# Quadrant moves of four tiles at once instead of two, with an order of transfers made for it

## The chip, the cores and the metric

One core of one Trainium2 chip. The metric is device microseconds of the whole kernel, as the median of its runs; "span" is the profiled stretch from the first to the last instruction, some 1.9 us shorter.

## The reference

```python
# x (16, 512, 1024), weight (1024, 768), add_value (16, 512, 768), all float32
def reference(x, weight, scale, add_value):
    return (scale * np.matmul(x, weight) + add_value).astype(np.float32)
```

Flattened, x has 8192 rows: 64 tiles of 128 rows. Each tile needs its x transposed and rounded to bf16, sixteen matmuls, and one VectorE instruction that scales the product and adds.

## The kernel before

SyncE issues all transfers in the order of one list. `x` are loads of x into 16 slots, `w` the weight, `a` loads of add_value into 32 slots, `o` stores of the results from the same 32 slots; the numbers are first tile and count.

```python
STREAM = [
    ("x", 0, 3), ("w", 0, 2), ("w", 2, 2), ("x", 3, 1), ("w", 4, 4), ("a", 0, 8),
    ("x", 4, 4), ("x", 8, 8), ("a", 8, 8), ("x", 16, 8), ("a", 16, 8), ("x", 24, 8),
    ("a", 24, 8), ("o", 0, 8), ("x", 32, 8), ("o", 8, 8), ("a", 32, 8), ("x", 40, 8),
    ("o", 16, 8), ("a", 40, 8), ("x", 48, 8), ("o", 24, 8), ("a", 48, 8), ("x", 56, 8),
    ("o", 32, 8), ("a", 56, 8), ("o", 40, 8), ("o", 48, 8), ("o", 56, 5), ("o", 61, 3),
]
```

From tile 14 on, x is not transposed on TensorE. ScalarE and GpSimd move blocks of 32 partitions to other partitions and round to bf16 on the way ("quadrant moves", two tiles at a time); one VectorE stream transpose then turns the 32 x 32 blocks.

```python
    def move_pair(t0, half):
        ...
        for b in range(4):
            for a, move in ((2 * half, nc.scalar.copy), (2 * half + 1, nc.gpsimd.tensor_copy)):
                move(moved[t0][32 * b:32 * b + 32, :, a, :],
                     src[32 * a:32 * a + 32, :, b, :])
        ...
    def turn_moved(t0):
        xt = xt_pool.tile([P, 2, KC, P], fp32, tag="xt")
        ...
        nc.vector.transpose(
            xt.rearrange("p i c m -> p (i c m)"),
            moved.pop(t0).bitcast(fp32).rearrange("p c a k -> p (c a k)"))
    ...
    def step():
        t = done["step"]
        if t < T - 1:
            for j in range(KJ):
                if j == KJ // 2:
                    if t + 1 not in in_pair:
                        transpose(t + 1)          # PE transposes, evacuated by VectorE
                    cast_to(min(t + AHEAD, done["x"] - 1))
                    for half in range(2):
                        if in_pair.get(t + 6 - half) == t + 6 - half:
                            move_pair(t + 6 - half, half)
                product(t, j, BOTH)
            finish(t, BOTH[0], 0, N)              # out = scale * product + add, in the add slot
            if in_pair.get(t + 4) == t + 4:
                turn_moved(t + 4)
    ...
    def added(t):                                 # tiles 0 to 2: their scaled product waits for add
        nc.vector.tensor_add(
            ao[:, t, :], ao[:, EARLY_AT + t, :], ao[:, t, :])
```

## Time and profile before

Median 210.29 us of three runs (210.13 to 210.51), span 208.4 us.

| From the page of the kernel before | |
|---|---|
| PE busy | 177.1 us (85%) |
| ScalarE busy, of which moves | 129.9 us (62%), 123.2 us |
| GpSimd busy, of which moves | 135.2 us (65%), 121.7 us |
| VectorE busy | 104.1 us (50%) |
| Share of the 16 DMA engines' span | 97.9%, for 87.03 MB |

How to read it: a share of busy time is an average, so the slices and the windows are needed to see whether a resource is full all the time or only in places. The lines themselves stand in the prediction below. "Issue to landing" is the time from SyncE's issue of a transfer until its landing is reported; where it is much longer than the bytes need, the transfer stood in a queue. The queue is "dry" when nothing is left in it. The "granted clock" is the share of its full speed at which TensorE was let run, as the profile records it.

### The profile page before, as it was taken

The page shows a single profiled execution, that of the slowest core. Times are in us where ns is not written, and L with a number is a line of the kernel's source. Part 1 is how long each engine was busy: PE and PEld are TensorE (multiplying, and loading weights), DVE is VectorE, ACT ScalarE, POOL GpSimd, SP SyncE. Part 2 cuts the span into 40 slices and gives each one's busy share as a digit, 9 for nine tenths or more (in the row PEclk, how much of TensorE's full clock was granted, in tenths as well). Part 3 has the DMA queues.
Part 4 walks back from the last instruction along what each step waited for, and adds up shares of the span by engine and source line. Part 5 has one row for each costly group of instructions (what it writes and reads, how often), then busy time and mean ns, then how long its engine had stood idle before and what let it go on. Part 6 is the DMA issues. An engine that isn't in the chain of part 4 may idle for free.

```text
span 208.4 us, 2843 instructions
## 1 busy us (share of the span) xinstructions
PE 177.1 (85%) x1059; PEld 108.4 (52%) x1080; DVE 104.1 (50%) x113; ACT 129.9 (62%) x210; POOL 135.2 (65%) x219
## 2 busy tenths in 40 slices
PE   0498339999999999999999999999959996799930
PEld 0355125666666666666666666666626563456510
DVE  0514713555675555566666645475054651555620
ACT  2421100540299999997999559992899919996000
POOL 1310051428699999999999759993899939997000
PEclk9999958999999999999999999999999999999995
DMA  6999999999999999999999999999999999999994
GB/s 229 413 440 448 420 459 406 440 453 415 402 464 434 413 415 425 458 415 428 415 439 451 407 436 425 450 428 407 439 426 437 453 404 426 434 437 425 423 414 187
DMA packets 4461, 87.21 MB, mean 418 GB/s; under 512 B 480, under 2 KB 480, under 8 KB 1120
## 3 DMA queue, kind: packets, MB, share of 16 engines
q1 hardware_dynamic: 4448, 87.03, 97.9%
q8 instruction: 8, 0.13, 0.2%
q14 instruction: 5, 0.04, 0.0%
HBM read 61.87 MB, written 25.17 MB: 418 GB/s over the span
## 4 chain that ended last, share of the span: by engine, by line
DMA 44%; PE 38%; POOL 10%; SPq 1%; issue 1%; DVE 1%; POOLq 0%; DVEq 0%
PE mm L170 36%; DMA out_dram<-ao 17%; DMA ao<-in_add_value_dram 15%; DMA xs<-in_x_dram 12%; POOL va L110 9%; PE tp L149 2%; DVE ao L178 1%; SPq L93 1%; SPq L250 1%; POOL xb L139 1%; SPq L256 0%; POOLq L139 0%; DVEq L178 0%
## 5 line engine op out<-in xcount | busy, mean ns | idle before, releaser
L170 PE MATMUL mm<-w_bf,xt 128*128 128x512 bf16 (+1 forms) x1003 | 170.6, 327 | 8.3 <-DVE ao L178 6.0
L110 ACT CAST va<-xs 32x512 bf16<-32x512 f32 x200 | 123.2, 616 | 46.0 <-DMA xs<-in_x_dram 43.5
L170 PEld LDWEIGHTS <-xt 128*128 128x128 bf16 x1024 | 101.0, 99 | 74.8 <-issue 5.5
L110 POOL CAST va<-xs 32x512 bf16<-32x512 f32 x200 | 121.7, 608 | 20.8 <-DMA xs<-in_x_dram 11.9
L178 DVE SCALAR_TENSOR_TENSOR ao<-mm,ao 128x768 f32<-128x768 f32 (+2 forms) x62 | 57.2, 935 | 40.3 <-PE mm L170 34.0
L119 DVE STREAM_TRANSPOSE xt<-va 128x1024 f32<-128x1024 f32 x25 | 31.1, 1244 | 29.5 <-POOL va L110 29.0
L139 POOL CAST xb<-xs 128x1024 bf16<-128x1024 f32 x11 | 11.2, 1043 | 29.4 <-DMA xs<-in_x_dram 21.8
L149 PE MATMUL tp<-identity,xb 128*128 128x128 f32 x56 | 10.2, 317 | 14.5 <-DVE xb L135 7.7
L149 PEld LDWEIGHTS tp<-identity,xb 128*128 128x128 f32 x56 | 7.7, 163 | 16.4 <-issue 7.7
L157 DVE COPY xt<-tp 128x1024 bf16<-128x1024 bf16 x10 | 6.9, 688 | 10.8 <-PE tp L149 10.8
L157 ACT COPY xt<-tp 128x512 bf16<-128x512 bf16 (+1 forms) x7 | 4.1, 655 | 9.2 <-PE tp L149 9.2
L97 DVE CAST w_bf<-ao 128x768 bf16<-128x768 f32 x8 | 4.0, 555 | 4.9 <-DMA ao<-in_weight_dram 4.9
L135 DVE CAST xb<-xs 128x512 bf16<-128x512 f32 x3 | 1.9, 695 | 7.1 <-DMA xs<-in_x_dram 7.1
L137 POOL CAST xb<-xs 128x512 bf16<-128x512 f32 x2 | 1.6, 835 | 5.9 <-DMA xs<-in_x_dram 5.9
L137 ACT CAST xb<-xs 128x512 bf16<-128x512 f32 x1 | 0.6, 619 | 5.1 <-DMA xs<-in_x_dram 5.1
L237 DVE TENSOR_TENSOR ao<-ao 128x768 f32<-128x768 f32 x3 | 2.7, 953 | 1.1 <-DMA ao<-in_add_value_dram 1.1
L206 DVE TENSOR_SCALAR ao<-mm 128x768 f32<-128x768 f32 x2 | 1.8, 953 | 2.5 <-PE mm L170 2.5
L137 ACT ACT_TABLE_LOAD x1 | 1.3, 1283 | 0.7 <-PEq L281 0.7
L203 ACT ACTIVATE ao<-mm 128x768 f32<-128x768 f32 x1 | 0.8, 817 | 0.0
masks.py:197 POOL MEMSET identity<- 128x128 f32 x1 | 0.2, 205 | 0.3 <-POOLq L281 0.3
masks.py:199 POOL TENSOR_SCALAR_AFFINE_SELECT identity<-identity 128x128 f32<-128x128 f32 x1 | 0.3, 293 | 0.1
L281 POOL MEMSET const-float32-0.0<- 128x1 f32 x1 | 0.1, 98 | 0.2 <-issue 0.2
(3 smaller groups left out, 0.3 us busy)
## 6 DMA issues: line engine op xcount, KB each, us to landing
xs<-in_x_dram SPq DMA_DIRECT2D x7, 4096.0 KB, 23.9
ao<-in_add_value_dram SPq DMA_DIRECT2D x8, 3072.0 KB, 31.1
out_dram<-ao SPq DMA_DIRECT2D x7, 3072.0 KB, 31.3
xs<-in_x_dram SPq DMA_DIRECT2D x1, 2048.0 KB, 24.4
out_dram<-ao SPq DMA_DIRECT2D x1, 1920.0 KB, 9.9
xs<-in_x_dram SPq DMA_DIRECT2D x1, 1536.0 KB, 6.4
ao<-in_weight_dram SPq DMA_DIRECT2D x2, 768.0 KB, 8.5
ao<-in_weight_dram SPq DMA_DIRECT2D x1, 1536.0 KB, 13.2
```

The source lines that it names most:

```text
L93: nc.sync.dma_start(ao[:, s:s + n, :].rearrange("p (c r) n -> p c (r n)", r=2), w_v[:, j // 2:(j + n) // 2, :])
L97: nc.vector.tensor_copy(w_bf[:, j + i, :], ao[:, s + i, :])
L110: move(moved[t0][32 * b:32 * b + 32, :, a, :], src[32 * a:32 * a + 32, :, b, :])
L119: nc.vector.transpose(xt.rearrange("p i c m -> p (i c m)"), moved.pop(t0).bitcast(fp32).rearrange("p c a k -> p (c a k)"))
L137: other(xb[:, K // 2:K], src[:, K // 2:K])
L139: nc.gpsimd.tensor_copy(xb, src)
L149: nc.tensor.transpose(tp[:, c, :], pairs[:, c * P:(c + 1) * P], identity)
L157: evacuate(xt_tiles[t][:, c:c + q, :].bitcast(bf16), tp[:, c:c + q, :].bitcast(bf16))
L170: nc.tensor.matmul(mm_tiles[t, cols[0]][:, n0:n1], lhs(t, j), w_bf[:, j, n0:n1], start=(j == 0), stop=(j == KJ - 1))
L178: nc.vector.scalar_tensor_tensor(a, mm_tiles[t, part][:, n0:n1], float(scale), a, op0=mybir.AluOpType.mult, op1=mybir.AluOpType.add)
L237: nc.vector.tensor_add(ao[:, t, :], ao[:, EARLY_AT + t, :], ao[:, t, :])
L250: nc.sync.dma_start(xs[:, k:k + n, :], rows(x_v, s, n))
```

## The change

The intent: the same bytes moved by half as many, twice as long instructions (each has a fixed part that is then paid half as often), x slots that come free in fours, and a list of 31 transfers that brings x earlier against add and out and splits the last load of x and the stores at the end anew. One buffer of moved tiles goes (three of two tiles become two of four).

```diff
--- before.py
+++ after.py
@@ -10,11 +10,12 @@
 
 
 STREAM = [
-    ("x", 0, 3), ("w", 0, 2), ("w", 2, 2), ("x", 3, 1), ("w", 4, 4), ("a", 0, 8),
-    ("x", 4, 4), ("x", 8, 8), ("a", 8, 8), ("x", 16, 8), ("a", 16, 8), ("x", 24, 8),
-    ("a", 24, 8), ("o", 0, 8), ("x", 32, 8), ("o", 8, 8), ("a", 32, 8), ("x", 40, 8),
-    ("o", 16, 8), ("a", 40, 8), ("x", 48, 8), ("o", 24, 8), ("a", 48, 8), ("x", 56, 8),
-    ("o", 32, 8), ("a", 56, 8), ("o", 40, 8), ("o", 48, 8), ("o", 56, 5), ("o", 61, 3),
+    ("x", 0, 3), ("w", 0, 2), ("w", 2, 2), ("x", 3, 1), ("w", 4, 4), ("x", 4, 4),
+    ("a", 0, 8), ("x", 8, 8), ("a", 8, 8), ("x", 16, 8), ("a", 16, 8), ("o", 0, 8),
+    ("x", 24, 8), ("a", 24, 8), ("x", 32, 8), ("a", 32, 8), ("o", 8, 8), ("x", 40, 8),
+    ("o", 16, 8), ("a", 40, 8), ("x", 48, 8), ("o", 24, 8), ("a", 48, 8), ("x", 56, 4),
+    ("a", 56, 8), ("x", 60, 4), ("o", 32, 8), ("o", 40, 8), ("o", 48, 8), ("o", 56, 6),
+    ("o", 62, 2),
 ]
 
 X_SLOTS = 16
@@ -25,7 +26,7 @@
 
 
 
-MOVED = [14, 16, 18, 20, 22, 24, 26, 28, 30, 32, 34, 36, 38, 40, 42, 44, 46, 48, 50, 52, 54, 56, 58, 60, 62]
+MOVED = [12, 16, 20, 24, 28, 32, 36, 40, 44, 48, 52, 56, 60]
 
 
 @with_exitstack
@@ -69,7 +70,7 @@
     const = ctx.enter_context(tc.tile_pool(name="const", bufs=1))
     xb_pool = ctx.enter_context(tc.tile_pool(name="xb_pool", bufs=XB_BUFS))
     xt_pool = ctx.enter_context(tc.tile_pool(name="xt_pool", bufs=3))
-    va_pool = ctx.enter_context(tc.tile_pool(name="va_pool", bufs=3))
+    va_pool = ctx.enter_context(tc.tile_pool(name="va_pool", bufs=2))
     tp_pool = ctx.enter_context(
         tc.tile_pool(name="tp_pool", bufs=2, space=bass.MemoryType.PSUM))
     mm_pool = ctx.enter_context(
@@ -83,8 +84,8 @@
     w_bf = const.tile([P, KJ, N], bf16, name="w_bf")
 
     xb_tiles, xt_tiles, mm_tiles, done = {}, {}, {}, {"cast": 0, "step": 0, "x": 0}
-    in_pair = {t0 + i: t0 for t0 in MOVED for i in range(2)}
-    moved, cast_pairs = {}, set()
+    in_four = {t0 + i: t0 for t0 in MOVED for i in range(4)}
+    moved, cast_fours = {}, set()
 
     def load_w(j, n):
 
@@ -96,35 +97,35 @@
         for i in range(n):
             nc.vector.tensor_copy(w_bf[:, j + i, :], ao[:, s + i, :])
 
-    def move_pair(t0, half):
-
-
-        if half == 0:
-            va = va_pool.tile([P, 2 * KC, 4, 64], bf16, tag="va")
+    def move_four(t0, b):
+
+
+        if b == 0:
+            va = va_pool.tile([P, 4 * KC, 4, 64], bf16, tag="va")
             moved[t0] = va
         k = t0 % X_SLOTS
-        assert k + 1 < X_SLOTS
-        src = xs[:, k:k + 2, :].rearrange("p i (c b k) -> p (i c) b k", b=4, k=64)
-        for b in range(4):
-            for a, move in ((2 * half, nc.scalar.copy), (2 * half + 1, nc.gpsimd.tensor_copy)):
-                move(moved[t0][32 * b:32 * b + 32, :, a, :],
-                     src[32 * a:32 * a + 32, :, b, :])
-        if half == 1:
-            cast_pairs.add(t0)
-
-    def turn_moved(t0):
+        assert k + 3 < X_SLOTS
+        src = xs[:, k:k + 4, :].rearrange("p i (c b k) -> p (i c) b k", b=4, k=64)
+        for a in range(4):
+            move = nc.scalar.copy if a % 2 == 0 else nc.gpsimd.tensor_copy
+            move(moved[t0][32 * b:32 * b + 32, :, a, :], src[32 * a:32 * a + 32, :, b, :])
+        if b == 3:
+            cast_fours.add(t0)
+
+    def turn_pair(t):
         xt = xt_pool.tile([P, 2, KC, P], fp32, tag="xt")
         for i in range(2):
-            xt_tiles[t0 + i] = xt[:, i, :, :]
+            xt_tiles[t + i] = xt[:, i, :, :]
+        t0 = in_four[t]
+        va = moved[t0].bitcast(fp32)[:, (t - t0) * KC:(t - t0 + 2) * KC, :, :]
         nc.vector.transpose(
-            xt.rearrange("p i c m -> p (i c m)"),
-            moved.pop(t0).bitcast(fp32).rearrange("p c a k -> p (c a k)"))
+            xt.rearrange("p i c m -> p (i c m)"), va.rearrange("p c a k -> p (c a k)"))
 
     def cast_to(t):
         while done["cast"] <= t:
             i = done["cast"]
-            if i in in_pair:
-                assert in_pair[i] in cast_pairs
+            if i in in_four:
+                assert in_four[i] in cast_fours
                 done["cast"] += 1
                 continue
             if len(xb_tiles) == XB_BUFS:
@@ -215,16 +216,16 @@
         if t < T - 1:
             for j in range(KJ):
                 if j == KJ // 2:
-                    if t + 1 not in in_pair:
+                    if t + 1 not in in_four:
                         transpose(t + 1)
                     cast_to(min(t + AHEAD, done["x"] - 1))
-                    for half in range(2):
-                        if in_pair.get(t + 6 - half) == t + 6 - half:
-                            move_pair(t + 6 - half, half)
+                    for b in range(4):
+                        if in_four.get(t + 8 - b) == t + 8 - b:
+                            move_four(t + 8 - b, b)
                 product(t, j, BOTH)
             finish(t, BOTH[0], 0, N)
-            if in_pair.get(t + 4) == t + 4:
-                turn_moved(t + 4)
+            if t + 4 in in_four and t % 2 == 0:
+                turn_pair(t + 4)
         else:
             for cols in BOTH:
                 for j in range(KJ):
```

## The prediction

> **What bounds the kernel now.** I read the page's slices first, because they say whether one resource is full from end to end.
>
> ```profile
> PE   0498339999999999999999999999959996799930
> ...
> DMA  6999999999999999999999999999999999999994
> GB/s 229 413 440 448 420 459 406 440 453 415 402 464 434 413 415 425 458 415 428 415 439 451 407 436 425 450 428 407 439 426 437 453 404 426 434 437 425 423 414 187
> ...
> q1 hardware_dynamic: 4448, 87.03, 97.9%
> ```
>
> The reader is to see that the DMA row is full in every slice but the first and the last, while PE has an early hole and two late dents. The transfers' bytes are the problem's own: x 33.55 MB, weight 3.15, add_value 25.17, out 25.17, together 87.03 MB, each moved once. Next I asked for stretches, to see whether the rate depends on what is being moved. Columns: the five engines' busy time with counts, granted clock, DMA share, GB/s.
>
> ```profile
> 40.00:60.00 20.00, 19.84 (x132) 13.26 (x134) 11.84 (x15) 7.85 (x14) 13.82 (x21) 1.00 1.00 427
> 60.00:100.00 40.00, 39.74 (x244) 24.09 (x247) 24.38 (x24) 37.87 (x62) 37.22 (x62) 1.00 1.01 431
> 100.00:140.00 40.00, 39.74 (x244) 24.10 (x247) 22.44 (x23) 35.08 (x58) 34.35 (x57) 1.00 1.00 431
> 140.00:180.00 40.00, 34.14 (x206) 20.38 (x209) 18.40 (x19) 30.64 (x51) 30.61 (x51) 1.00 1.00 430
> 180.00:200.00 20.00, 19.33 (x117) 11.34 (x117) 11.59 (x13) 10.77 (x18) 10.98 (x19) 1.00 0.99 425
> 200.00:208.40 8.40, 0.00 (x0) 0.00 (x0) 0.29 (x1) 0.00 (x0) 0.00 (x0) 0.73 0.64 274
> ```
>
> From 40 to 200 us the rate is 425 to 431 GB/s at share 1.00, with loads alone (40 to 60), with both directions (60 to 180), and mostly stores at the end. PE's dents do not show in it. So the queue of transfers, not PE, ScalarE or GpSimd, sets the length. The chain of waits gives PE matmuls 36.1%, which misleads: it follows semaphores, and a transfer that was issued early and queued behind others looks like no wait at all.
>
> A saturated queue can hide a late issue only while others are still queued. So the last two issues come next, from SyncE's timeline and the DMA issues of the end (last figure: us from issue to landing):
>
> ```profile
> 194.81 0.33 SPq L264 DMA_DIRECT2D out_dram<-ao  x1
> ...
> 200.32 0.33 SPq L264 DMA_DIRECT2D out_dram<-ao  x1
> ```
> ```profile
> out_dram<-ao SPq DMA_DIRECT2D x1, 1920.0 KB, 9.9
> out_dram<-ao SPq DMA_DIRECT2D x1, 1152.0 KB, 7.1
> ```
>
> The five-tile store issued at 194.81 lands at 204.7; the three-tile store issued at 200.32 lands at 207.4. Alone it would need 1.18 MB / 430 = 2.7 us, and 204.7 + 2.7 = 207.4: it stood in the queue behind its predecessor for 4.4 us. Even the last issue is not on the path.
>
> Last, SyncE's waits, the long ones:
>
> ```profile
> SPq L250 <- ACT va L110: 63.7, 5, 19.5
> SPq L264 <- DVE ao L178: 41.8, 4, 22.5
> SPq L256 <- DMA out_dram<-ao: 34.0, 4, 9.6
> ```
>
> They look like what the change attacks (loads of x waiting for moves that empty the slots), but they are waits of the issuer with transfers still queued behind it: issue to landing has a median of 24 to 31 us in the page, for transfers of which a 4.19 MB one takes only 9.8 us.
>
> **What the Trainium skill says.** "DMA: Bandwidth & Descriptors", Specifications, gives a fabric ceiling of 435 GB/s. The trace's 431 is 99% of it, so it agrees, and the rate has nothing left to give. (The same table's limit of about 358 GB/s for HBM per core is exceeded here.) The page's "Anatomy of one DMA" says that DMA engines do not wait on semaphores, the issuing sequencer does; the trace agrees: SyncE waits 63.7 us on ScalarE's moves while the DMA share stays 1.00. "ScalarE: Activation LUTs", What ACT_TABLE_LOAD costs, has 186 ns + 0.833 ns per element for an instruction with immediates: 612 ns at 512 elements, against 616 ns for the move in the trace. "GPSIMD Engine Reference", Engine selection, calls one-input work roughly line-rate; the rows below (608 ns beside 616) agree.
>
> **The change part by part.**
>
> ```profile
> L110 ACT CAST va<-xs 32x512 bf16<-32x512 f32 x200 | 123.2, 616 | 46.0 <-DMA xs<-in_x_dram 43.5
> L110 POOL CAST va<-xs 32x512 bf16<-32x512 f32 x200 | 121.7, 608 | 20.8 <-DMA xs<-in_x_dram 11.9
> L119 DVE STREAM_TRANSPOSE xt<-va 128x1024 f32<-128x1024 f32 x25 | 31.1, 1244 | 29.5 <-POOL va L110 29.0
> L139 POOL CAST xb<-xs 128x1024 bf16<-128x1024 f32 x11 | 11.2, 1043 | 29.4 <-DMA xs<-in_x_dram 21.8
> L157 ACT COPY xt<-tp 128x1024 bf16<-128x1024 bf16 x1 | 1.0, 1012 | 7.9 <-PE tp L149 7.9
> ```
>
> *Moves.* 25 pairs x 8 moves of 512 elements become 13 fours x 8 moves of 1024, on each of the two engines. A 1024-element instruction should take about 1.04 us on both: ScalarE 186 + 853 ns by the page's line, with the 1012 ns copy of this trace beside it, and GpSimd's 1024-element cast takes 1043 ns. So 104 x 1.04 = 108 us on each, against 123.2 and 121.7: some 14 us of busy time saved on either, though it covers two tiles more. Per eight tiles, with the gap of 0.04 us between moves, 16 x 1.08 = 17.3 us instead of 32 x 0.65 = 20.8. Transfers need 10.49 MB / 0.43 = 24.4 us for the same eight tiles. Neither figure is above that; the saving lies beside the queue. Worth to the end: 0.
>
> *Latency of a move.* A pair was ready 8 x 0.65 = 5.2 us after its x landed; a four needs 8 x 1.08 = 8.7 us before its first pair can be transposed. That is 3.5 us later for PE, once for each landing of x, and does not add up.
>
> *Tiles 12 and 13* leave the PE path: 8 PE transposes (2 x 0.44 us) and two evacuations of 688 ns go, one stream transpose of 1244 ns comes: 26 x 1.244 = 32.3 us on VectorE. GpSimd loses two casts (2.1 us). Nothing of it is on the path.
>
> *x 4-7 ahead of add 0-7.* The order on record lands x 4-7 at 28.1 us and add at 23.2; they swap, so x lands 3.15 MB / 0.43 = 7.3 us sooner, at 20.8. This fills PE's hole at 23 to 29 us. But tile 8 still waits for x 8-15, which lands at 39.0 either way, so PE is only some 3.5 us ahead, and the queue is no shorter.
>
> *Transfer order after that.* I replayed the new list by hand: a transfer lands at 4.8 us + (MB before and including it) / 0.4294, which puts the old list's last landing at 207.5; and a four takes 8.7 us, a stream transpose 1.25, a PE tile 2.65. A transfer costs time only when it is issued after the one ahead of it has landed. Issue, and landing of the one ahead: x 24-31 at 52 and 70.7 (after store 0-7); x 32-39 at 73.5 and 87.8; x 40-47 at 98 and 112; add 40-47 at 112 (waits for store 8-15) and 129; x 48-55 at 115 and 137; add 56-63 at 154 and 166; store 48-55 at 179 and 193; store 56-61 at 195 and 200; store 62-63 at 200.5 and 205.7. The smallest margin is some 5 us, at the end, as before (5.4 and 4.4).
>
> *Tail.* Both lists end with stores that are queued. In the new one x 60-63 lands at 178.2; the four is ready at 186.9, transposed at 188.1, and four tiles of PE end near 199.5, where the old PE ended at 199.86. The last store is 0.79 MB instead of 1.18 MB, but its size matters only where it is not queued behind another. Gain 0 to 0.3 us.
>
> *Split load.* One transfer more, with the same bytes: under 0.1 us.
>
> Sum: 210.29 - 0.15 + 0.05 = **210.2 us**.
>
> **The rivals.** (1) *The moves are the bound, and 14 us less of them shows.* For: 9 of 10 busy in many slices on both engines, GpSimd's moves on the chain of waits, 63.7 us of SyncE's waits. Against: the DMA share is 1.00 while they run. Were it right, the time would fall toward the floor: 87.03 MB / 435 = 200.1 us at the page's ceiling, plus some 3 us of start, some 1 us of end and the 1.9 us between span and time, about 206; the best case is a hair at 2%. (2) *The queue runs dry.* Store 0-7 now stands ahead of x 24-31, so a late tile 7 would hold a load; two va buffers instead of three, and a four ready 3.5 us later, could stack up. For: SyncE issues strictly in its order. Against: margins of 12 us and more in the middle. A four slower than I think (1.3 us a move) would use 14 us instead of 8.7 and eat the end's 5 us: 211 to 214 us. (3) *The tail gets shorter by more than I say,* because the fastest DMA engines run dry before the last store comes (274 GB/s in the last 8.4 us). For: the slices taper. Against: the end is the slowest engine's, which is queued. Worth at most 1 us: 209.3.
>
> **Range and chances.** The before runs span 0.4 us. Rival 3 gives the low side, 209.4; a margin eaten at the end gives the high side, 211.2. Faster by over 2% needs 206.1, which asks for the whole floor: 0.02. Slower by over 2% needs 4.2 us of dry queue: 0.03. Within 2%: 0.95.
>
> **What would show it right or wrong.** Right: 104 moves on each engine at about 1.04 us and 108 us in sum; DMA share 1.00 and 430 GB/s through 40 to 200 us; PE's hole before 29 us shorter; the last store landing 5 to 8 us after its issue. Wrong: a stretch below 415 GB/s in the middle, a last store landing about 4 us after its issue (nothing queued ahead of it), or moves above 1.2 us.

## The result, and the profile after

210.34 us median (210.07 to 210.82, six runs) against 210.22 for the kernel before (six runs). The ratio is 1.0006, 95% interval 0.9993 to 1.0019: the same. A ratio here is the mean time of one kernel's fast runs over the mean of the other's in the same rounds, so it isn't quite the ratio of the medians quoted.

The slices of the page after:

```profile
PE   0598609999699999989999999999967999999930
...
DMA  6999999999999999999999999999999999999994
...
q1 hardware_dynamic: 4592, 87.03, 98.0%
```

The DMA row is the same, digit for digit. PE's early hole is still there, one slice long (the 0 in the sixth place). The stretches (busy of PE, PE's weight loads, VectorE, ScalarE, GpSimd with counts; granted clock, DMA share, GB/s):

```profile
60.00:100.00 40.00, 38.85 (x237) 23.44 (x240) 21.52 (x22) 31.20 (x31) 30.73 (x31) 1.00 1.01 431
100.00:140.00 40.00, 39.74 (x243) 24.09 (x247) 22.90 (x24) 31.51 (x31) 31.58 (x31) 1.00 1.00 431
140.00:180.00 40.00, 36.69 (x224) 22.12 (x227) 22.53 (x23) 26.60 (x26) 26.32 (x26) 1.00 1.01 430
...
200.00:208.40 8.40, 0.00 (x0) 0.00 (x0) 0.24 (x1) 0.00 (x0) 0.00 (x0) 0.70 0.62 265
```

ScalarE and GpSimd have some 6.5 us less to do from 60 to 100 (37.87 and 37.22 before) and some 3 us less from 100 to 140 (35.08 and 34.35 before), and the rate of the transfers is what it was: 431, 431, 430 GB/s. The groups of instructions (busy us, mean ns; idle time before them and what ended it):

```profile
L111 ACT CAST va<-xs 32x1024 bf16<-32x1024 f32 x104 | 108.5, 1043 | 56.9 <-DMA xs<-in_x_dram 55.5
L111 POOL CAST va<-xs 32x1024 bf16<-32x1024 f32 x104 | 107.6, 1034 | 36.1 <-DMA xs<-in_x_dram 31.6
```

The saving is real: 123.2 to 108.5 us on ScalarE, 121.7 to 107.6 on GpSimd. It went into waiting: before the moves, the idle time that x's arrival ended rose from 43.5 to 55.5 us on ScalarE and from 11.9 to 31.6 us on GpSimd. The engines do the work faster and then wait longer for the same queue. SyncE's long waits, after:

```profile
SPq L265 <- DVE ao L179: 59.5, 6, 18.5
SPq L257 <- DMA out_dram<-ao: 48.6, 3, 22.6
SPq L251 <- ACT va L111: 46.3, 4, 23.5
```

Loads of x wait less for ScalarE's moves (46.3 us, 63.7 before), and stores and loads of add wait more: the issuer's waits change places, while earlier transfers are still queued all the time. And the end, from SyncE's timeline and from the DMA issues after 193 us:

```profile
195.60 0.33 SPq L265 DMA_DIRECT2D out_dram<-ao  x1
...
200.26 0.33 SPq L265 DMA_DIRECT2D out_dram<-ao  x1
```
```profile
out_dram<-ao SPq DMA_DIRECT2D x1, 2304.0 KB, 9.9
out_dram<-ao SPq DMA_DIRECT2D x1, 768.0 KB, 7.1
```

The last store is issued within 0.06 us of the old one's time and lands 7.1 us later, as before, although it is two tiles and not three: it is queued, so its own length doesn't matter.

### The profile page after: what moved, and what is told of

Its sections match the earlier page's. It is cut to its first block, busy times and chain, and to the rows that moved or that the text cites. A ratio compares the mean times of both kernels' runs of the same rounds, so it can differ in the third digit from the quotient of the medians.

```text
span 208.3 us, 2643 instructions
## 1 busy us (share of the span) xinstructions
PE 176.5 (85%) x1051; PEld 107.6 (52%) x1072; DVE 102.6 (49%) x112; ACT 115.2 (55%) x114; POOL 119.1 (57%) x121
## 4 chain that ended last, share of the span: by engine, by line
DMA 60%; PE 16%; POOL 13%; DVE 3%; SPq 2%; issue 1%; POOLq 1%
DMA xs<-in_x_dram 42%; DMA out_dram<-ao 18%; PE mm L171 16%; POOL va L111 11%; POOL xb L140 2%; DVE ao L179 1%; DVE xt L121 1%; SPq L251 1%; SPq L94 1%; POOLq L296 1%; SPq L257 0%; POOLq L111 0%; POOLq L140 0%
## 5 line engine op out<-in xcount | busy, mean ns | idle before, releaser
L171 PE MATMUL mm<-w_bf,xt 128*128 128x512 bf16 (+1 forms) x1003 | 170.8, 328 | 15.6 <-DVE xt L158 8.9
L111 ACT CAST va<-xs 32x1024 bf16<-32x1024 f32 x104 | 108.5, 1043 | 56.9 <-DMA xs<-in_x_dram 55.5
L111 POOL CAST va<-xs 32x1024 bf16<-32x1024 f32 x104 | 107.6, 1034 | 36.1 <-DMA xs<-in_x_dram 31.6
L121 DVE STREAM_TRANSPOSE xt<-va 128x1024 f32<-128x1024 f32 x26 | 32.1, 1236 | 36.2 <-POOL va L111 36.2
L140 POOL CAST xb<-xs 128x1024 bf16<-128x1024 f32 x9 | 9.2, 1041 | 25.7 <-DMA xs<-in_x_dram 22.1
L150 PE MATMUL tp<-identity,xb 128*128 128x128 f32 x48 | 8.9, 323 | 7.7 <-DVE xb L136 7.4
L150 PEld LDWEIGHTS tp<-identity,xb 128*128 128x128 f32 x48 | 6.9, 168 | 9.3 <-issue 7.6
L158 DVE COPY xt<-tp 128x1024 bf16<-128x1024 bf16 x8 | 5.5, 686 | 7.1 <-PE tp L150 7.1
```

The costliest lines, as they stand in the source:

```text
L111: move(moved[t0][32 * b:32 * b + 32, :, a, :], src[32 * a:32 * a + 32, :, b, :])
L121: nc.vector.transpose(xt.rearrange("p i c m -> p (i c m)"), va.rearrange("p c a k -> p (c a k)"))
L140: nc.gpsimd.tensor_copy(xb, src)
L150: nc.tensor.transpose(tp[:, c, :], pairs[:, c * P:(c + 1) * P], identity)
L158: evacuate(xt_tiles[t][:, c:c + q, :].bitcast(bf16), tp[:, c:c + q, :].bitcast(bf16))
L171: nc.tensor.matmul(mm_tiles[t, cols[0]][:, n0:n1], lhs(t, j), w_bf[:, j, n0:n1], start=(j == 0), stop=(j == KJ - 1))
```

## The experiments

The theory, Q: the queue of transfers is never empty from about 3 us to the end, and everything the change does lies behind it. Its rivals: O, the two parts of the change have effects that cancel; M, the moves set the pace and something else took their gain; L, an addition to Q: the fours make each first pair later, and the full queue hides that.

### The parts one at a time

`order_only` is the kernel before with the new list; `fours_only` is the changed kernel with the old list. The diff is in each case the STREAM alone.

> The kernel before with the new order of 31 transfers alone; the moves stay in pairs with three buffers. Theory Q (the queue of transfers is full from 3 to 207 us and sets the time): 210.2 us, ratio 0.998 to 1.002, DMA share 1.00 through 40 to 200 us. Rival O (the two parts of the change cancel, the order losing or winning something that the fours give back): a ratio further than 0.5% from 1, and the opposite sign in the run with the fours alone.

> The changed kernel with the old order of 30 transfers; the moves in fours. Theory Q: 210.2 to 210.8 us. By the replay x 56-63 lands as one at 170.8, the last four is ready at 188.2, PE ends near 201 and the last store of three tiles goes out near 201.6, with its predecessor landing at 204.7: still queued, but by 3 us only. Rival O: a ratio further than 0.5% from 1, opposite in sign to the order alone.

Measured: `order_only` 210.42 us, ratio 0.9996 (0.9982 to 1.0010). `fours_only` 210.74 us, ratio 1.0028 (0.9996 to 1.0061), its six runs from 210.32 to 212.37. O falls: neither part's ratio is 0.5% from 1 (the interval of `fours_only` reaches 0.6%), and the order's interval contains 1, so there is nothing of note to cancel. But the two differ in how close the queue comes to running dry. The last store in the DMA issues of the end, first `order_only`, then `fours_only`:

```profile
out_dram<-ao SPq DMA_DIRECT2D x1, 768.0 KB, 9.3
```
```profile
out_dram<-ao SPq DMA_DIRECT2D x1, 1152.0 KB, 4.1
```

9.3 us from issue to landing means a long queue ahead; 4.1 us for 1.18 MB (2.7 us of bytes) means next to none: the DMA share had fallen to 0.15 from 203.5 to 204.5 us. In `fours_only` the last store went out at 203.78 and not at 201.6 as I expected. I had let PE go on while the last eight tiles were awaited; in the trace PE stops for 2.37 us until 182.33 (x 56-63 landed at 171.4, a four takes 8.7, the transpose 1.25, and a finish), and eight tiles of 2.64 us from there end at 203.3. So the fours alone use up the margin at the end; the new order, which splits that last load in two, gives it back.

### Is the end really set by queued stores?

`after_tail8` joins the last two stores of the changed kernel:

```diff
-    ("a", 56, 8), ("x", 60, 4), ("o", 32, 8), ("o", 40, 8), ("o", 48, 8), ("o", 56, 6),
-    ("o", 62, 2),
+    ("a", 56, 8), ("x", 60, 4), ("o", 32, 8), ("o", 40, 8), ("o", 48, 8), ("o", 56, 8),
```

> The changed kernel with its last two stores (six tiles and two) made one of eight. It can go out only after tile 63, at 200.3, when the one ahead of it has landed (200.1). Theory Q: the queue is dry there, so the store's own time and its start show: 3.15 MB / 0.43 = 7.3 us after some 2 us, landing near 209.7: 212.4 us (211.8 to 213.5), a ratio of 1.010. A theory in which the last store's time isn't what counts (the end is set by something after it): 210.3.

Measured: 212.1 us (211.63 to 212.99), ratio 1.0099 (1.0071 to 1.0128). From SyncE's timeline and the DMA issues:

```profile
200.96 0.33 SPq L264 DMA_DIRECT2D out_dram<-ao  x1
```
```profile
out_dram<-ao SPq DMA_DIRECT2D x1, 3072.0 KB, 8.7
```

Issued at 200.96, 8.7 us to landing, on an empty queue: 7.3 us of bytes and 1.4 us of start and report, where I had put some 2. The same bytes that cost nothing while queued cost 2 us once a store has to wait for the last tile.

### Fewer bytes: does the time follow them?

Both kernels, with the last two loads of add_value cut to half their tiles (wrong results, relative error 0.37):

```diff
-            nc.sync.dma_start(ao[:, k:k + n, :], rows(add_v, s, n))
+            m = n // 2 if s >= 48 else n
+            nc.sync.dma_start(ao[:, k:k + m, :], rows(add_v, s, m))
```

> The kernel before, with the last two loads of add_value cut to half their tiles (wrong result on purpose for eight tiles): 3.15 MB less to move, 7.3 us at 0.4294 MB per us. Theory Q: the queue's end comes at 200.2 instead of 207.5; PE, which was held by x 56-63 and by add 56-63, ends near 196.5, so the last store is just about queued: 203.2 us (202.7 to 204.5). A theory in which PE or the moves set the time: under 2 us gained, above 208.

> The changed kernel with the same cut. Theory Q with a second part, L (a four is ready 3.5 us later than the first pair was, which the full queue hid): PE runs without a hole from 157.6 (it waits there for the first four of x 48-55, which the cut doesn't bring forward) to 199.7, so the store of tiles 56-61 goes out near 195.6 on a dry queue and the last one at 200.2: 206 to 207.7 us, 3 to 4 us above the kernel before with the same cut. Without L: 203.2 as the other.

Measured: the kernel before 204.85 us (203.23 to 205.04), ratio 0.9732 (0.9693 to 0.9771); the changed one 207.6 us (206.44 to 208.58), ratio 0.9891 (0.9838 to 0.9943). Both get faster with the bytes, which speaks for Q and against M, and the kernel before gains 5.6 us (2.68% of 210.09) of the 7.3 that the bytes are worth; I had said 203.2, and 204.85 is just over my limit. The cut also brings x 56-63 forward (all of it has landed at 167.3 instead of 170.8 us in the kernel before, at 171.2 instead of 178.3 in the changed one), from which a kernel paced by PE or by the moves could gain too. In the changed kernel that isn't the gain: PE ends at 199.5 us with the cut and at 199.8 without, and only the stores end sooner. In the kernel before PE ends 2.6 us sooner, less than half of the gain. What ended the gain is PE. Each kernel's timeline of PE and its last store in the DMA issues, first the kernel before, then the changed one:

```profile
153.83 43.44 PE L170 MATMUL mm<-w_bf,xt 128*128 128x512 bf16 x256 [2.89 <-DVE ao L178]
```
```profile
out_dram<-ao SPq DMA_DIRECT2D x1, 1152.0 KB, 4.2
```
```profile
157.71 41.76 PE L171 MATMUL mm<-w_bf,xt 128*128 128x512 bf16 x256 [2.61 <-DVE ao L179]
```
```profile
out_dram<-ao SPq DMA_DIRECT2D x1, 768.0 KB, 4.1
```

In the kernel before the store ahead had landed 0.4 us before the last one went out. In the changed one the DMA share is 0.00 from 193 to 195.5 us, until PE is far enough for the store of tiles 56 to 61 (issued at 195.29), and the last store stands behind that one alone. So the queue runs dry in both before PE is done. PE comes out of its wait for x 48-55 at 153.83 with pairs and at 157.71 with fours, 3.9 us later (x itself landed 0.4 us later there), and from there it is PE that sets the end. That is L: 1.6% between the two ratios, 3.3 us. PE's timeline in `order_only` and in `fours_only` shows that the fours make it and not the order:

```profile
154.41 43.44 PE L171 MATMUL mm<-w_bf,xt 128*128 128x512 bf16 x251 [2.33 <-DVE ao L179]
```
```profile
157.58 22.38 PE L170 MATMUL mm<-w_bf,xt 128*128 128x512 bf16 x126 [2.68 <-DVE ao L178]
```

From the landing of x 48-55 (146.95 and 146.68 us) that is 7.5 us with pairs and 10.9 us with fours, the same as in the two kernels with the cut. The latency that the fours add is there and is hidden in the kernel as it stands.

### What the change did buy

If the moves have margin, then added moves cost nothing until the margin is used, and the kernel with cheaper moves should bear more. Each kernel repeats some of its moves of 512 elements on both engines (the same data written twice, so the results are right). The larger dose, first the pairs, then the fours:

```diff
-                move(moved[t0][32 * b:32 * b + 32, :, a, :],
-                     src[32 * a:32 * a + 32, :, b, :])
+                for again in range(2 if b == 0 else 1):
+                    move(moved[t0][32 * b:32 * b + 32, :, a, :],
+                         src[32 * a:32 * a + 32, :, b, :])
```
```diff
             move(moved[t0][32 * b:32 * b + 32, :, a, :], src[32 * a:32 * a + 32, :, b, :])
+            if a < 2:
+                h = 2 * KC
+                move(moved[t0][32 * b:32 * b + 32, 0:h, a, :], src[32 * a:32 * a + 32, 0:h, b, :])
```

> The kernel before, with two more moves of 512 elements per pair on ScalarE and on GpSimd (the same data written twice, result right). Per eight tiles: 40 moves x 0.652 = 26.1 us, against 24.4 us that the transfers of eight tiles take. Theory Q: the moves are now the longer of the two, 24 pairs x 6.52 = 156.5 us from x 16-23's landing at 56 us, then two tiles and a store on a dry queue: about 226 us (221 to 229). Rival M (the moves were the bound all along, so that added moves show one for one): 25 x 1.3 = 33 us more, about 243 us.

> The changed kernel with the same work added: four more moves of 512 elements per four and engine (the same data written twice, result right). Per eight tiles 16 x 1.08 + 8 x 0.652 = 22.5 us, still under the 24.4 us of the transfers. Theory Q: 210.3 to 212 us: the last four is ready at 189.5 instead of 187, PE ends near 202, the last store is still queued. Rival M: 13 x 2.6 = 34 us more, about 244 us. Rival D (the fours have made the margin too thin): over 214 us.

Then half the dose, on both (`b == half == 0` in the pairs; `a < 2 and b % 2 == 0` in the fours), and on the pairs with the new order:

> The kernel before with one more move of 512 elements per pair and engine (result right): half of the dose that cost it 18.1 us. The moves then take 5.87 us per pair, 23.5 per eight tiles. Working from the last landing of x (170.8 us): four pairs end at 194.3, transpose 1.25, two tiles of PE 5.3, finish 1: 202, and the store ahead of the last lands at 204.7, so the last is still queued: 210.2 to 211. If cost followed the dose (half of 18.1), 219. If the true margin is smaller than I read, 211 to 214.

> The changed kernel with two more moves of 512 elements per four and engine (result right): half of the dose that cost it 4.3 us. A four then takes 8 x 1.083 + 2 x 0.652 = 9.97 us. Working from the loads, which come every 19.5 us per eight tiles from 81 to 178.6 us and not every 24.4 as I had it: ten fours from 81 end at 180.7 at the earliest, so landings set the pace again; the last four lands at 178.4, is ready at 188.4, PE ends near 201.5, the store ahead lands at 205.5: still queued, 210.2 to 210.9. If cost followed the dose (half of 4.3), 212.4.

> The new order of transfers with moves in pairs and the dose of one more move of 512 elements per pair and engine (result right): which part of the change bought the margin? Theory F (the fours did, by taking less time per tile): GpSimd again works without a break, now from the landing of x 24-31, which this order brings at 81 us instead of 73: 20 pairs x 5.9 = 118, so 199, PE ends near 206.5, the last store of two tiles goes out near 207 on a dry queue and lands 4.1 us later: 213 to 214.5 us, a little worse than the old order with this dose (212.2). Theory O (the order did): 210.2 to 210.8.

| Added moves of 512 per two tiles and engine | pairs, old order | pairs, new order | fours, new order |
|---|---|---|---|
| none | 1 (210.2 us) | 0.9996 (210.42) | 1.0006 (210.34) |
| 1 | 1.0097 (212.21) | 1.0220 (214.83) | 0.9996 (210.12) |
| 2 | 1.0859 (228.6) | not run | 1.0193 (214.6) |

The intervals are 1.0082 to 1.0113, 1.0205 to 1.0235 and 0.9984 to 1.0009 at the half dose, and 1.0838 to 1.0880 and 1.0177 to 1.0210 at the full one. M falls at once: 15.7 us more of moves on GpSimd (26 of 605 ns) leave the changed kernel at the same time. The kernel before has less room: the half dose costs it 2 us. The order alone does not bring the room: with pairs in the new order the same dose costs 4.6 us, 0.3 us more than I had allowed. The fours alone were not given a dose. In the old order they run dry at the end without one (`fours_only`), so the changed kernel's room most likely needs both parts; shown is only that it needs the fours. One line of the timelines of each shows the pace under a dose that hurts: PE in `before_load`, PE in `after_load`, GpSimd in `order_load1`.

```profile
156.65 5.36 PE L171 MATMUL mm<-w_bf,xt 128*128 128x512 bf16 x32 [1.20 <-DVE ao L179]
163.22 5.36 PE L171 MATMUL mm<-w_bf,xt 128*128 128x512 bf16 x31 [1.20 <-DVE ao L179]
```
```profile
162.50 10.56 PE L174 MATMUL mm<-w_bf,xt 128*128 128x512 bf16 x63 [0.75 <-DVE ao L182]
173.81 10.56 PE L174 MATMUL mm<-w_bf,xt 128*128 128x512 bf16 x63 [0.76 <-DVE ao L182]
```
```profile
81.33 118.23 POOL L112 CAST va<-xs 32x512 bf16<-32x512 f32 x180 [1.72 <-DMA xs<-in_x_dram]
```

PE does two tiles in 5.36 us and starts the next two 6.57 us after: the 1.2 us between is a wait for a pair, ten moves at some 0.655. In the fours PE does four tiles in 10.56 us every 11.31. In the third GpSimd works 118 us without a break. The wait line names VectorE's finish: PE needs the PSUM buffer that this instruction frees, and on VectorE it stands behind the stream transpose, which waits for the moves. The chain behind such a line is longer than the line tells.

Two of the expectations, `before_load1` and `after_load`, were off for one reason; in the second, what I had set down as rival D (over 214 us) came true. I compared the moves of eight tiles with the 24.4 us of transfers for eight tiles. But loads of x do not come evenly. In the old order x 16-23 and x 24-31 land at 56 and 73 us, 17 us apart; in the new one x 24-31 and x 32-39 at 81 and 98. Moves of 23.5 us (pairs, half dose) fall 6.5 us behind there and win back only 0.9 us with every later group, so on GpSimd, which works from 53.5 to 197.5 us without a break, they are still behind when the last x lands (ScalarE, a little faster, waits 1.6 us for that x): PE ended at 205.0 in `before_load1` and not at 202. Likewise the full dose on the fours (22.6 us per eight tiles) worked without a break from 81 us: ten fours of 11.31 end at 194.2, PE at 207, the queue had run dry before the last two stores (DMA share 0.00 from 202 to 203.5 us), 214.6 us and not 210.3 to 212. The half dose on the fours (9.97 us per four, 20 per eight) came in as said; my text for it speaks of loads every 19.5 us, which is an average of unequal gaps too.

### Why PE's early hole stayed

The prediction said that x 4-7 ahead of add 0-7 fills PE's hole. It only moved the hole. From the timelines of VectorE and of PE in the changed kernel:

```profile
27.86 2.70 DVE L238 TENSOR_TENSOR ao<-ao 128x768 f32<-128x768 f32 x3 [5.95 <-DMA ao<-in_add_value_dram]
30.47 0.68 DVE L158 COPY xt<-tp 128x1024 bf16<-128x1024 bf16 x1
```
```profile
31.21 2.74 PE L171 MATMUL mm<-w_bf,xt 128*128 128x512 bf16 x8 [6.92 <-DVE xt L158]
```

In this trace VectorE takes its instructions in the order of the program. The three additions for tiles 0 to 2 stand ahead of the evacuation of tile 4's transposes (the copy of the transposed tile out of PSUM) and wait for add 0-7, which now lands at 27.8. PE had tile 4 transposed by 23 us and then waited 6.92 us for that evacuation. To test it, `after_late_added` puts the additions behind the finish of tile 5:

```diff
             finish(t, BOTH[0], 0, N)
+            while late and t >= 5:
+                added(late.pop(0))
...
-            for t in range(s, min(s + n, EARLY)):
-                added(t)
+            late.extend(range(s, min(s + n, EARLY)))
```

> The changed kernel, but VectorE's three additions for tiles 0 to 2, which wait for add 0-7 (27.8 us), stand behind the finish of tile 5 instead of ahead of the evacuation of tile 4. Theory: those additions are why PE's early hole moved (24 to 31 us) instead of filling. Expected: PE's wait for VectorE's evacuation falls from 8.9 us to under 5, the store of tiles 0-7 goes out at 43 to 44.5 us instead of 46.9, and the time stays within 0.3 us of the changed kernel, 210.3, since the queue is full there anyway. If the hole stays, the cause is another.

Measured: wrong result (relative error 0.22, not meant) and 226.18 us. The fault is the edit's. The scaled products of tiles 0 to 2 are kept in slots that add 16-23 fills, and that load now stood ahead of the additions in the program, so they waited for it (VectorE idle 28.0 us, until 63.3) and added the wrong data. It tells nothing of the time under test. The mended form keeps them in the slots that the weight has left and that add 24-31 fills next:

```diff
-    EARLY_AT = A_SLOTS - KJ - EARLY
+    EARLY_AT = A_SLOTS - KJ
```

> The mended form of the run with the late additions: the three scaled results of tiles 0 to 2 wait in slots that add 24-31 fills, not in slots that add 16-23 fills, so no load overwrites them (result right). Expected: PE's early hole ends at 28 to 29 us instead of 31.2, the store of tiles 0-7 goes out at 43 to 44.5 us instead of 46.9, and the time is that of the changed kernel within 0.5 us, 209.9 to 210.8, since the queue is full there. If the hole stays as it was, VectorE's order is not its cause.

Measured: right result, 210.28 us, ratio 1.0008 (0.9994 to 1.0021). PE's timeline around the hole:

```profile
25.83 1.46 PE L171 MATMUL mm<-w_bf,xt 128*128 128x512 bf16 x8
30.92 2.21 PE L171 MATMUL mm<-w_bf,xt 128*128 128x512 bf16 x8 [3.63 <-DVE xt L158]
```

PE now works through tile 4 and has its transposes of tile 5 done before it stops; its hole there falls from 6.92 to 3.63 us and the store of tiles 0 to 7 goes out at 44.3 us instead of 46.93. So the order on VectorE was part of the cause, by some 3 us. It isn't all: the hole ends at 30.9 and not at 28 to 29, because the finish of tile 3 stands in the same place and waits for the same load, which in this run landed at 29.2. Nor does PE keep what it wins: VectorE's first stream transpose waits for its moves and stands ahead of an evacuation, PE stops for 4.87 us until 54.23 (2.03 us until 54.01 in the changed kernel), and its waits for evacuations come to 9.7 us in all, against 8.9. And the time does not move, as Q has it.

## Why the prediction was right or wrong

*The bound.* Right. The DMA share stayed at 1.00, and the time follows bytes (`before_add48`) and not moves (`after_load2`).

*The moves.* Right: 104 of 1043 and 1034 ns against 1.04 us, 108 us in sum. Their gain is off the path; it shows up as idle time before the moves.

*The replay of the list.* Right to within 0.9 us at each issue that it named:

| Transfer | x 24-31 | x 32-39 | x 40-47 | add 40-47 | x 48-55 | add 56-63 | out 48-55 | out 56-61 | out 62-63 |
|---|---|---|---|---|---|---|---|---|---|
| predicted issue, us | 52 | 73.5 | 98 | 112 | 115 | 154 | 179 | 195 | 200.5 |
| measured | 52.13 | 73.21 | 98.39 | 112.61 | 115.67 | 153.98 | 179.86 | 195.60 | 200.26 |

*The latency of a four.* Right, 3.5 us said and 3.4 seen (10.9 against 7.5 us from landing to PE); it costs time where the queue is dry and is hidden otherwise. That it "does not add up" held by a hair. GpSimd in the changed kernel, from the landing of x 24-31:

```profile
81.15 34.50 POOL L111 CAST va<-xs 32x1024 bf16<-32x1024 f32 x32 [7.96 <-DMA xs<-in_x_dram]
```

Eight tiles take it 17.2 us, and x 32-39 lands 17.0 us after x 24-31, so it goes from the one to the other without a wait. With 22.6 us (`after_load`) the delay does add up.

*x 4-7 ahead of add 0-7.* Wrong, in "This fills PE's hole at 23 to 29 us". The step left out the order of instructions on VectorE: the hole moved to 24 to 31 us and is no shorter (6.92 us of wait, 6.45 before). The sign "PE's hole before 29 us shorter" came true only in that PE now works 1.3 us of the stretch from 23 to 29. It cost nothing for the reason that the same paragraph gave, that the queue is no shorter for it.

*"Neither figure is above that; the saving lies beside the queue."* Right in its verdict, but the comparison of 17.3 us with 24.4 is too kind. The gap between two loads of x is once 17 us, and a dose experiment showed that pairs had less room than the 24.4 suggests: 23.5 us per eight tiles already cost 2 us. What counts is the backlog: undosed pairs, at 20.8 us, also fall behind at that gap (GpSimd works 62.7 us without a break from 56.08) but have caught up when x 40-47 lands at 121.85.

*The tail.* The gain of 0 to 0.3 us did not come: the difference lies inside 0.1%. Rival 1 is refuted by the dose. Rival 2 did not happen, and its size was told too small: a four of 14 us was to give 211 to 214, and one of 11.3 gave 214.6. The prediction counted the longer four once, at the end; under the dose the delay added up from one landing to the next. Rival 3 was not seen.

What stays open: why `fours_only` and the two kernels with fewer bytes spread over some 2 us from run to run (and `after_tail8` over 1.4), where most others hold some 0.5. In all of them the queue runs dry before the end, but so it does in the dosed kernels, which don't spread. And the some 3 us at the start and 1 us after the last landing were not tried. As no variant with a right result beat 210 us by more than the noise, there is no better version to show.

## What to carry to other kernels

Where the slices show the transfers full from end to end, look at the time from issue to landing of the last transfers: well above what their bytes need, the queue hides everything ahead of it, and faster engines only wait longer. A change that doesn't move the time may still have bought margin, and a dose of added work, or fewer bytes, shows how much. Margin is read from the backlog that the shortest gap between two arrivals leaves, and from whether the longer gaps work it off before the end, not from the average gap.

## What the Trainium skill lacked or had wrong

- "DMA: Bandwidth & Descriptors", Specifications: the row with about 358 GB/s as the limit of HBM per core, which the prediction calls exceeded, does not say that it is meant for two cores that stream from one HBM at once; the page says so only further down, under "Measured". For this kernel on one core the runs show 427 GB/s with loads alone (40 to 60 us of the kernel before) and 430 to 431 with loads and stores over 120 us; the page's fabric ceiling of 435 is the one that held.
- The same page, Anatomy of one DMA, gives about 2.0 us of fixed cost, for the GpSimd path, and the page has no such total for transfers that SyncE issues. For stores that SyncE issued on a dry queue the runs show 4.2 us for 1.18 MB (`before_add48`), 6.9 us for 2.36 MB (`after_add48`, the store ahead of the last) and 8.7 us for 3.15 MB (`after_tail8`); less 2.7, 5.5 and 7.3 us of bytes at 0.43 MB per us, that leaves 1.4 to 1.5 us in each.
- "GPSIMD Engine Reference", Engine selection, calls one-input work roughly line-rate. The page has no duration and no fixed part of a one-input copy or cast. The moves took 608 ns at 512 and 1034 ns at 1024 elements on 32 partitions: 0.83 ns an element and some 182 ns fixed, nearly ScalarE's 616 and 1043.
